# Second feed-forward matrix by seven block products per block of four, with operands summed beside the first matrix

## The chip, the core and the metric

The kernel runs on one core of a Trainium2 chip. The metric is the device time of one execution in microseconds (us). Three runs of the kernel before gave 3480.54, 3479.45 and 3491.56 us, median 3480.54 us. The engines are called as in the profile: PE is TensorE (matrix products), PEld its weight load, DVE VectorE, ACT ScalarE, POOL GpSimd, and SP the engine that here only issues DMA transfers.

## What is computed

One inference step of an encoder of two layers over 1056 tokens (1024 frames of a new stream and 32 of a running one). A layer mixes three kinds of attention, attends to a memory, and ends in a squared-ReLU feed forward between two norms:

```python
D_MODEL = 1024
DEPTH = 2
D_FF = 4 * D_MODEL
...
    x = layer_norm(ALPHA * x + memory_attention(x, mem_k, mem_v, w_xq, w_xo), ln_g[1], ln_b[1])
    ffn = jnp.square(jax.nn.relu(x @ w_ff1)) @ w_ff2
    x = layer_norm(ALPHA * x + ffn, ln_g[2], ln_b[2])
```

So the first matrix is 1024 by 4096, the second 4096 by 1024, both in each layer, in 32-bit floats.

## The kernel before

Activations lie transposed: features on the 128 partitions, tokens along the row, T = 1056. Every 32-bit product is three matmuls on rounded parts (`mm3`, L98 to L102): an operand x is split (`split`, L94 to L96) into hi, a rounded copy made by ACT (L95), and lo = x − hi, made by DVE (L96); the product is hi·hi + hi·lo + lo·hi. A raw weight chunk of 128x512 (256 KB) comes by a DMA on SP into a tile tagged "ws" (two buffers), and ACT and DVE split it into tiles "wu" (ring "w" of eight).

**First matrix** (`ffn_up`, L1419 to L1472). The 1024 inputs and the tokens are halved, which makes four blocks of the operand; the 4096 outputs go in 16 steps j of 256. In each j the eight block products are had from seven (the Strassen-Winograd scheme): `first_blocks` and `mix_blocks` (L1371 ff.) form the seven operands X once per layer, `mix_weights` (L1400 to L1417) sums the weights of every j: S1 and S2 on DVE (L1413, L1414), S3 and S4 on POOL (L1416, L1417), and splits all seven. A product is 24 matmuls of 128x264 (two halves of 264 tokens, four row blocks, three matmuls each). Results are combined on DVE (L1438, L1454), then made relu and squared on ACT (L1441, L1442), and stored to a DRAM buffer `hid` by DMAs on POOL's queue (L1444). A raw tile of mixed weights ("u" ring of large tiles, shared with Y) is loaded at L1404 and L1405.

**Second matrix** (`ffn_down`, L1474 to L1501). The 4096 rows go in eight groups: a group loads four hid rows from DRAM (SP), splits them, and multiplies with the weights of all eight output blocks in three chunks of 352 tokens (L100 to L102, `add_proj`, which adds into Y on DVE, L1212 and L1214). The last group goes chunk by chunk, with the second norm of the layer behind each chunk.

**Order.** A tile framework gives each engine its list by its own planner: instructions of one engine run in that order, and wait for semaphores of the others. SP alone keeps the order of the program. Tiles come from small pools of buffers, so a load also waits until its buffer's last reader is through.

## Time and profile before

| | us |
|---|---|
| runs | 3480.54, 3479.45, 3491.56 |
| profiled execution | 3483.91 |
| its span in the trace | 3482.1 |
| PE busy | 3318.6 (95%) |
| DVE busy | 2055.3 (59%) |
| ACT busy | 1524.9 (44%) |
| POOL busy | 464.6 (13%) |
| mean granted TensorE clock | 0.977 of full |

The page and the trace describe the one profiled execution. Busy is time in which an engine worked; register, branch, semaphore and DMA-issuing instructions don't count. A stretch's PEclk is the share of the full TensorE clock that was granted: 1.00 is 2.4 GHz, 0.50 is 1.2 GHz. In layer 1 the feed forward starts near 1015 us and its second matrix near 1362 us; layer 2 repeats this some 1700 us later.

### The profile page before, as it was taken

What the parts mean: (1) busy time and instruction counts of PE and PEld (TensorE: products, weight loads), DVE (VectorE), ACT (ScalarE), POOL (GpSimd) and SP (SyncE); (2) the same over time, 40 slices, a digit from 0 to 9 for tenths busy, and PEclk for the clock granted to TensorE, in tenths of its full rate; (3) what the DMA queues carried; (4) which work ended last, traced back from release to release, by engine and by line L of the source; (5) the groups of instructions that cost most, each with busy time, mean ns of one, the idle gap of its engine ahead of it and who ended that gap; (6) DMA issues with size and microseconds to landing.
All of it is one profiled execution on the core that took longest, in us unless ns stands there. A gap on an engine that the chain in (4) does not pass through costs nothing.

```text
span 3482.1 us, 61117 instructions
## 1 busy us (share of the span) xinstructions
PE 3318.6 (95%) x23904; PEld 3084.8 (89%) x23904; DVE 2055.3 (59%) x4223; ACT 1524.9 (44%) x3312; POOL 464.6 (13%) x722
## 2 busy tenths in 40 slices
PE   8999999999979999999989999999999799999998
PEld 6988879689879999999989887786898799999997
DVE  5666742566587665444656677335666866654446
ACT  5555533554555544221254554335544545431113
POOL 0101023110013221000011111221000232200000
PEclk9999999999989999999999999999999899999999
DMA  4424236432313334322143332455422233352221
GB/s 161 135 54 119 70 129 207 126 118 92 133 54 123 112 108 168 105 99 93 45 133 95 88 98 68 139 175 136 145 95 91 95 107 110 106 190 87 80 99 57
DMA packets 196425, 386.83 MB, mean 111 GB/s; under 512 B 46240, under 2 KB 98120, under 8 KB 195880
## 3 DMA queue, kind: packets, MB, share of 16 engines
q1 hardware_dynamic: 119600, 248.66, 22.8%
q0 software_dynamic: 41056, 125.63, 10.3%
q10 hardware_dynamic: 35480, 8.64, 1.3%
q8 instruction: 189, 3.10, 0.4%
q14 instruction: 100, 0.82, 0.1%
HBM read 259.60 MB, written 123.23 MB: 110 GB/s over the span
## 4 chain that ended last, share of the span: by engine, by line
PE 76%; DVE 7%; DMA 6%; issue 6%; ACT 3%; POOL 1%; SPq 0%; ACTq 0%; another core or an unknown queue 0%; DVEq 0%; POOLq 0%
PE psw L100 16%; PE psw L101 16%; PE psw L102 16%; PE pso L792 2%; PE pss L785 2%; PE pso L100 2%; PE pso L102 2%; PE pso L101 2%; PE pss L101 2%; PE pss L102 2%; PE pso L161 2%; PE pss L100 2%; DMA Gb<-gd 1%; DVE X L96 1%; PE pst L100 1%
## 5 line engine op out<-in xcount | busy, mean ns | idle before, releaser
L100 PE MATMUL psw<-X,wu 128*128 128x352 f32 (+1 forms) x2496 | 806.0, 323 | 33.2 <-ACT X L95 24.2
L101 PE MATMUL psw<-X,wu 128*128 128x352 f32 (+1 forms) x2496 | 798.2, 320 | 8.2 <-DVE X L96 8.0
L102 PE MATMUL psw<-X,wu 128*128 128x352 f32 (+1 forms) x2496 | 799.1, 320 | 4.4 <-DVE wu L96 4.1
L100 PEld LDWEIGHTS psw<-X,wu 128*128 128x128 f32 x2496 | 477.5, 191 | 44.0 <-ACT X L95 25.2
L100 PE MATMUL psw<-hid,wu 128*128 128x352 f32 x1536 | 500.2, 326 | 7.3 <-ACT wu L95 5.3
L101 PE MATMUL psw<-hid,wu 128*128 128x352 f32 x1536 | 498.7, 325 | 0.0
L102 PE MATMUL psw<-hid,wu 128*128 128x352 f32 x1536 | 497.7, 324 | 0.0
L101 PEld LDWEIGHTS psw<-X,wu 128*128 128x128 f32 x2496 | 476.5, 191 | 14.7 <-DVE X L96 9.5
L102 PEld LDWEIGHTS psw<-X,wu 128*128 128x128 f32 x2496 | 477.2, 191 | 7.7 <-DVE wu L96 5.4
L95 ACT CAST wu<-ws 128x512 fp32r<-128x512 f32 x304 | 182.3, 619 | 525.5 <-PE psw L101 379.7
L1214 DVE TENSOR_TENSOR Y<-psw,Y 128x352 f32<-128x352 f32 x336 | 175.3, 523 | 294.0 <-PE psw L102 290.9
L100 PEld LDWEIGHTS psw<-hid,wu 128*128 128x128 f32 x1536 | 289.8, 189 | 8.9 <-ACT wu L95 5.7
L101 PEld LDWEIGHTS psw<-hid,wu 128*128 128x128 f32 x1536 | 290.6, 189 | 0.5
L102 PEld LDWEIGHTS psw<-hid,wu 128*128 128x128 f32 x1536 | 289.8, 189 | 0.7
L96 DVE TENSOR_TENSOR wu<-ws,wu 128x512 fp32r<-128x512 f32 x304 | 204.6, 688 | 119.2 <-ACT wu L95 95.2
L96 DVE TENSOR_TENSOR wu<-wraw,wu 128x512 fp32r<-128x512 f32 x224 | 195.5, 878 | 77.1 <-ACT wu L95 77.0
L95 ACT CAST wu<-wraw 128x512 fp32r<-128x512 f32 x224 | 136.1, 617 | 158.2 <-PE pst L102 38.7
L180 ACT ACTIVATE lnq<-Y 128x352 f32<-128x352 f32 x168 | 76.9, 492 | 176.2 <-DVE Y L177 156.4
L1441 ACT ACTIVATE ff<-ff 128x528 f32<-128x528 f32 (+1 forms) x160 | 88.3, 554 | 122.2 <-DVE ff L1454 88.9
L1444 POOL DMA_DIRECT2D hid<-ff x160 | 87.1, 544 | 403.3 <-ACT ff L1442 270.2
L100 PE MATMUL pss<-X,wu 128*128 128x264 f32 x448 | 128.5, 288 | 3.1 <-ACT X L95 3.1
L101 PE MATMUL pss<-X,wu 128*128 128x264 f32 x448 | 128.6, 287 | 1.7 <-DVE X L96 1.7
(540 smaller groups left out, 6909.6 us busy)
## 6 DMA issues: line engine op xcount, KB each, us to landing
hid<-hid SPq DMA_DIRECT2D x64, 528.0 KB
wraw<-in_w_ff_dram SPq DMA_DIRECT2D x64, 512.0 KB
ws<-in_w_ff_dram SPq DMA_DIRECT2D x128, 256.0 KB
ws<-in_w_in_dram SPq DMA_DIRECT2D x100, 256.0 KB
hid<-ff POOLq DMA_DIRECT2D x96, 264.0 KB, 3.8
xd<-Y POOLq DMA_DIRECT2D x24, 704.0 KB, 3.9
Y<-xd SPq DMA_DIRECT2D x24, 704.0 KB
foxd<-fb POOLq DMA_DIRECT2D x24, 352.0 KB, 3.6
```

Source lines behind the costliest of these rows:

```text
L95: self.nc.scalar.copy(hi, src)
L96: (eng or self.nc.vector).tensor_sub(lo, src, hi.bitcast(F32))
L100: mm(ps, lhs[0], rhs[0], start=first, stop=False)
L101: mm(ps, lhs[0], rhs[1], start=False, stop=False)
L102: return mm(ps, lhs[1], rhs[0], start=False, stop=last)
L161: total = lambda ps, x, k=0, n=1: nc.tensor.matmul(ps[:, :CW], self.o1024, x, start=k == 0, stop=k == n - 1)
L180: nc.scalar.activation(q, y(k), AF.Square)
L785: nc.tensor.transpose(pt[:, c:c + 128], Ps[h][:, 128 * k:128 * k + 128], self.ident)
L792: nc.tensor.matmul(po[64 * h:64 * h + 64, 0:128], V[k][:, 64 * h:64 * h + 64], PT[:, k - k0, h], start=k == 0, stop=k == kts - 1)
L1214: nc.vector.tensor_add(y, ps, y)
L1441: nc.scalar.activation(x, x, AF.Relu)
L1444: nc.gpsimd.dma_start(self.hid[2 * j + i, :, n * HT + c * QT:n * HT + c * QT + m], x.rearrange("p c n -> p (c n)"))
```

## The change

The second matrix is done by seven block products too. Of the 16 pairs of its row blocks (outputs j of the first matrix), 14 (`FAST`) go this way; the last four hid rows are multiplied as before. In `ffn_down`, each of seven operands of 14 blocks of 528 tokens meets the four column blocks m: 14 · 3 · 2 = 84 matmuls of 128x264 for each, and the result is added into one to four blocks of Y (`to`).

- The operands are sums of results of the first matrix. They are formed in `ffn_up` by DVE right after the results, stored to a DRAM buffer `tp` (seven operands) by DMAs on ACT's queue and SP's, and read back by `down_operand`. `hid` shrinks to four rows and is stored through ACT's queue.
- The weight sums for the second matrix are made on POOL by `down_sums`: for each j from 2 on and each m a 256 KB load into a "ws" buffer, four sums of 128x128, and a 256 KB store into a buffer `sp`; 56 of them per layer. They are issued after the last operand sum of the first matrix (`issue_after`).
- S3 and S4 of the first matrix's weights move from POOL to DVE. The raw weights are loaded one j ahead.
- Products 0 and 1 of j = 0 to 3 (`EARLY`) are done ahead, in `ffn_first`, from unmixed operands; their results go to DRAM through POOL's queue and come back on SP's, and `ffn_up` has five products in those j. The order of products is now 0, 1, 2, 3, 6, 4, 5.
- Y is loaded back inside `ffn_down` in eight pieces; Xn is allocated at the first norm.

Over both layers 4032 matmuls of 128x352 go and 4704 of 128x264 come.

```diff
+FAST = 14
+EARLY = 4
...
-        sub(B21, B21, B22, self.nc.gpsimd)
+        for h in halves:
+            self.after = self.nc.gpsimd.tensor_sub(B21[:, h], B21[:, h], B22[:, h]).ins
...
+    def mix_weights(self, raw, first=False):
+        nc = self.nc
...
+        W = [None, None] if first else [split(A11), split(A12)]
         nc.vector.tensor_add(S1, A21, A22)
         nc.vector.tensor_sub(S2, S1, A11)
         W += [split(S2), split(S1)]
-        nc.gpsimd.tensor_sub(S3, A11, A21)
-        nc.gpsimd.tensor_sub(S4, A12, S2)
+        nc.vector.tensor_sub(S3, A11, A21)
+        nc.vector.tensor_sub(S4, A12, S2)
...
+    def ffn_first(self, l, X):
+        nc = self.nc
+        self.hid = self.dram("hid", [32 - 2 * FAST, 128, T])
+        self.tp = self.dram("tp", [7, FAST, 128, HT])
+        self.sp = self.dram("sp", [4, 4, 128, FAST, 128])
+        self.p1d = self.dram("p1d", [EARLY, 128, 2, QT])
+        for j in range(EARLY):
+            W = self.k3(self.unit(self.I["w_ff1"][l, 2 * j]), 8)
+            ps = self.block_product(lambda k: [a[:, k] for a in W], X[0])
+            p1 = self.tl("q", [128, 2, QT], name="ff")
+            for c in range(2):
+                nc.scalar.copy(p1[:, c], ps[c])
+            nc.gpsimd.dma_start(self.p1d[j], p1)
+            ps = self.block_product(lambda k: [a[:, 4 + k] for a in W], X[1])
+            c11 = self.tl("q", [128, 2, QT], name="ff")
+            for c in range(2):
+                nc.vector.tensor_add(c11[:, c], ps[c], p1[:, c])
+            self.squared(c11)
+            nc.gpsimd.dma_start(self.tp[0, j], c11.rearrange("p c n -> p (c n)"))
...
+    def down_sums(self, l, j):
+        eng = self.nc.gpsimd
+        last = None
+        def store():
+            if last:
+                eng.dma_start(self.sp[:, last[0], :, j].rearrange("s p n -> p s n"), last[1])
+        for m in range(4):
+            raw = self.tl("ws", [128, 4, 128], name="wb")
+            c0 = 512 * (m % 2) + 256 * (j % 2)
+            src = self.I["w_ff2"][l, j // 2, :, :, c0:c0 + 256].rearrange("(a u) p c -> u p a c", a=2)[m // 2]
+            eng.dma_start(raw.rearrange("p (a k) n -> p a (k n)", a=2), src)
+            store()
+            A11, A12, A21, A22 = (raw[:, i] for i in range(4))
+            eng.tensor_add(A22, A21, A22)
+            eng.tensor_sub(A21, A11, A21)
+            eng.tensor_sub(A11, A22, A11)
+            eng.tensor_sub(A12, A12, A11)
+            last = m, raw
+        store()
...
+                W = self.mix_weights(raw, j < EARLY)
+            if j < 15:
+                raw = self.raw_weights(I["w_ff1"][l, 2 * j + 2:2 * j + 4])
...
+                if j >= FAST:
+                    nc.scalar.dma_start(self.hid[2 * (j - FAST) + at[0], :, HT * at[1] + t0:HT * at[1] + t0 + n], flat(x))
+                elif i is not None:
+                    nc.scalar.dma_start(self.tp[i, j, :, t0:t0 + n], flat(x))
...
+            if j < EARLY:
+                nc.sync.dma_start(u, self.p1d[j])
+                for c in range(2):
+                    nc.sync.dma_start(flat(c11[c]), self.tp[0, j, :, c * QT:(c + 1) * QT])
+            else:
+                product(0)
+                for c in range(2):
+                    nc.scalar.copy(u[:, c], ps[c])
+                product(1)
+                for c in range(2):
+                    nc.vector.tensor_add(c11[c][:, 0], ps[c], u[:, c])
+                for c in range(2):
+                    square(c11[c], 0, (0, 0), c)
+            fast = j < FAST
+            product(2)
...
+            if fast:
+                for c in range(2):
+                    nc.vector.tensor_sub(c12[:, c], c12[:, c], c11[c][:, 0])
+                nc.sync.dma_start(self.tp[3, j], flat(c12))
+            product(4)
+            plus(c22, c22)
+            plus(u, u)
+            square(c22, 6, (1, 1))
+            if fast:
+                nc.vector.tensor_sub(c22, c22, c12)
+                nc.sync.dma_start(self.tp[2, j], flat(c22))
+                for c in range(2):
+                    nc.vector.tensor_sub(c11[c][:, 0], c22[:, c], c11[c][:, 0])
+                    nc.sync.dma_start(self.tp[4, j, :, c * QT:(c + 1) * QT], flat(c11[c]))
+            product(5)
+            plus(u, u)
+            square(u, 1, (1, 0))
+            if fast:
+                nc.vector.tensor_sub(u, u, c22)
+                nc.sync.dma_start(self.tp[5, j], flat(u))
+            if j >= 16 - FAST:
+                with self.tc.issue_after(self.after):
+                    self.down_sums(l, j - 16 + FAST)
...
+        def take(tile, n):
+            j = len(X)
+            lo, hi = tile
+            (self.nc.gpsimd if i else self.nc.sync).dma_start(lo.bitcast(F32), self.tp[i, j:j + n].rearrange("j p n -> p j n"))
+            for a in range(0, n, 2):
+                b = min(a + 2, n)
+                self.split(hi[:, a:b], lo[:, a:b], lo[:, a:b].bitcast(F32))
+            X.extend((hi[:, a], lo[:, a]) for a in range(n))
...
+                raw = self.tl("ws", [128, 4, 128], name="ws")[:, :b - a]
+                if i in (0, 1, 5):
+                    for k in range(a, b, 2):
+                        src = self.I["w_ff2"][l, (j0 + k) // 2, m // 2 + (i == 5) * 2]
+                        src = src.rearrange("p (m k e n) -> p m k e n", m=2, k=2, e=2)[:, m % 2, :, int(i > 0)]
+                        nc.sync.dma_start(raw[:, k - a:k - a + 2], src)
+                else:
+                    nc.sync.dma_start(raw, self.sp[{2: 0, 6: 1, 4: 2, 3: 3}[i], m, :, j0 + a:j0 + b])
+                self.split(hi[:, a:b], lo[:, a:b], raw)
...
+        to = [((0, 0), (0, 1), (1, 0), (1, 1)), ((0, 0),), ((0, 1), (1, 0), (1, 1)), ((0, 1), (1, 1)), ((1, 0), (1, 1)),
+              ((1, 0),), ((0, 1),)]
+        X = self.down_operand(0)
+        Y = None
+        for i in range(7):
+            for m in range(4):
+                W = self.down_weights(l, i, m)
+                if Y is None:
+                    Y = [self.tl("u", [128, 4, ROW], name="Y") for _ in range(2)]
+                    for k in range(4):
+                        for a in range(2):
+                            nc.sync.dma_start(Y[a][:, k, :T], xd[:, 4 * a + k])
+                if m == 0:
+                    Xn = self.down_operand(i + 1) if i < 6 else self.last_hid()
+                ps = {}
                 for c in range(2):
                     ps[c] = self.ps("wsowsowt"[self.nps % 8])[:, :QT]
                     self.nps += 1
...
+                    for k in range(FAST):
+                        self.mm3(ps[c], W[k], [x[:, c * QT:(c + 1) * QT] for x in X[k]], k == 0, k == FAST - 1)
+                for a, b in to[i]:
+                    for c in range(2):
+                        y = Y[a][:, m, HT * b + QT * c:HT * b + QT * (c + 1)]
+                        if i == 0:
+                            nc.vector.scalar_tensor_tensor(y, y, ALPHA, ps[c], ALU.mult, ALU.add)
+                        else:
+                            nc.vector.tensor_add(y, ps[c], y)
+            X = Xn
...
+        self.ffn_first(l, X)
+        W = self.mix_weights(self.raw_weights(I["w_ff1"][l, 0:2]), True)
```

Three places of the engines' lists follow; the changed kernel's line numbers are its own: L99 and L100 there are the two halves of `split`, L1505 is `plus`, L1421 to L1425 are S1 to S4.

POOL in layer 1 at the last operand sum before the first matrix (Y_9305 is half of the block sums, hid, tp and sp are DRAM buffers). Before:

```order
L1444 DMA hid_10405<-ff_10461 128x264
L1444 DMA hid_10405<-ff_10462 128x264
L1385 TENSOR_TENSOR Y_9305<-Y_9305 128x2x528 x2
L1444 DMA hid_10405<-ff_10525 128x528
L1416 TENSOR_TENSOR wraw_10624<-wraw_10624 128x512
L1444 DMA hid_10405<-ff_10526 128x528
L1444 DMA hid_10405<-ff_10432 128x528
L1417 TENSOR_TENSOR wraw_10624<-wraw_10624 128x512
L1416 TENSOR_TENSOR wraw_10870<-wraw_10870 128x512
```

After the change (L1397 is the operand sum, wb a "ws" tile):

```order
L1397 TENSOR_TENSOR Y_9305<-Y_9305 128x2x528
L1477 DMA wb_11245<-in_w_ff_dram 128x2x256
L1477 DMA wb_11251<-in_w_ff_dram 128x2x256
L1480 TENSOR_TENSOR wb_11245<-wb_11245 128x128
L1481 TENSOR_TENSOR wb_11245<-wb_11245 128x128
L1482 TENSOR_TENSOR wb_11245<-wb_11245 128x128
L1483 TENSOR_TENSOR wb_11245<-wb_11245 128x128
L1480 TENSOR_TENSOR wb_11251<-wb_11251 128x128
L1472 DMA sp_10340<-wb_11245 128x4x128
L1481 TENSOR_TENSOR wb_11251<-wb_11251 128x128
L1482 TENSOR_TENSOR wb_11251<-wb_11251 128x128
```

POOL's list was stores of results with a weight sum between them; it is now, from there on, pairs of load, load, eight sums, two stores.

DVE in layer 1 about the first steps j of the first matrix (ff are results, wraw raw weights and their sums, ps.. PSUM). Before, the combining of j = 0 and then the weights of j = 1:

```order
L1438 TENSOR_TENSOR ff_10526<-pso_10562,ff_10526 128x264
L1438 TENSOR_TENSOR ff_10526<-psw_10575,ff_10526 128x264
L1438 TENSOR_TENSOR ff_10432<-pss_10593,ff_10432 128x264
L96 TENSOR_TENSOR wu_10627<-wraw_10624,wu_10627 128x512
L1438 TENSOR_TENSOR ff_10432<-pso_10606,ff_10432 128x264
L96 TENSOR_TENSOR wu_10630<-wraw_10624,wu_10630 128x512
L1413 TENSOR_TENSOR wraw_10624<-wraw_10624 128x512
L1414 TENSOR_TENSOR wraw_10624<-wraw_10624 128x512
L1413 TENSOR_TENSOR wraw_10870<-wraw_10870 128x512
L96 TENSOR_TENSOR wu_10635<-wraw_10624,wu_10635 128x512
```

After the change (wraw_10691 holds the weights of j = 1; L1544 is a parked sum):

```order
L1421 TENSOR_TENSOR wraw_10691<-wraw_10691 128x512
L1424 TENSOR_TENSOR wraw_10691<-wraw_10691 128x512
L1505 TENSOR_TENSOR ff_10694<-psw_10700,ff_10694 128x264
L1505 TENSOR_TENSOR ff_10694<-pss_10713,ff_10694 128x264
L1505 TENSOR_TENSOR ff_10754<-pso_10728,ff_10694 128x264
L1505 TENSOR_TENSOR ff_10754<-psw_10741,ff_10694 128x264
...
L1544 TENSOR_TENSOR ff_10783<-ff_10783,ff_10696 128x264
L1505 TENSOR_TENSOR ff_10694<-psw_10830,ff_10694 128x264
L1422 TENSOR_TENSOR wraw_10691<-wraw_10691 128x512
L1505 TENSOR_TENSOR ff_10694<-pss_10843,ff_10694 128x264
L1425 TENSOR_TENSOR wraw_10691<-wraw_10691 128x512
L100 TENSOR_TENSOR wu_10865<-wraw_10691,wu_10865 128x512
```

S1 and S3 of j = 1 now stand ahead of the first results of j = 0, and S2, S4 and the splits of j = 1 between and behind its last results.

ACT in layer 1 at the end of the first matrix (wu<-ws are casts of the second matrix's weights). Before:

```order
L1441 ACTIVATE ff_14216<-ff_14216 128x528
L95 CAST hid_14334<-hid_14334 128x1056
L1442 ACTIVATE ff_14216<-ff_14216 128x528
L95 CAST hid_14334<-hid_14334 128x1056
L95 CAST wu_14342<-ws_14343 128x512
L1441 ACTIVATE ff_14122<-ff_14122 128x528
L95 CAST wu_14342<-ws_14347 128x512
L1442 ACTIVATE ff_14122<-ff_14122 128x528
```

After the change (X_14941 and X_14945 are row blocks of operand 1 of the second matrix, ff_14632 and ff_14631 among the first and the last results of j = 15):

```order
L1439 ACTIVATE ff_14632<-ff_14632 128x264
L99 CAST X_14941<-X_14941 128x528
L1440 ACTIVATE ff_14632<-ff_14632 128x264
L99 CAST X_14945<-X_14945 128x528
L1511 DMA hid_10338<-ff_14632 128x264
...
L1439 ACTIVATE ff_14631<-ff_14631 128x528
L1511 DMA hid_10338<-ff_14750 128x528
L1440 ACTIVATE ff_14631<-ff_14631 128x528
L99 CAST wu_14905<-ws_14906 128x512
L1511 DMA hid_10338<-ff_14631 128x528
L99 CAST wu_14905<-ws_14911 128x512
```

Casts of operand 1 now stand among the squares of j = 15, and the first weights of the second matrix behind the last square.

## Rows read from the trace of the kernel before

**Rows 1.** The page's head and its busy times by engine (share of the span, instructions).

```profile
span 3482.1 us, 61117 instructions
...
PE 3318.6 (95%) x23904; PEld 3084.8 (89%) x23904; DVE 2055.3 (59%) x4223; ACT 1524.9 (44%) x3312; POOL 464.6 (13%) x722
```

**Rows 2.** Windows, steady stretches: window, length, busy (count) of PE, PEld, DVE, ACT, POOL; clock, DMA, GB/s.

```profile
1150.00:1200.00 50.00, 50.00 (x412) 50.00 (x411) 29.32 (x54) 26.02 (x49) 12.76 (x17) 1.00 0.36 122
...
1100.00:1300.00 200.00, 200.00 (x1642) 200.00 (x1641) 125.57 (x229) 98.65 (x187) 54.62 (x68) 1.00 0.30 103
...
1420.00:1700.00 280.00, 280.00 (x1736) 279.92 (x1736) 130.03 (x217) 48.75 (x68) 0.00 (x0) 1.00 0.25 85
```

**Rows 3.** Windows, the start of the feed forward of layer 1.

```profile
1004.00:1015.00 11.00, 9.68 (x53) 7.56 (x52) 7.43 (x7) 6.17 (x11) 0.00 (x0) 1.00 0.14 52
1015.00:1027.00 12.00, 1.95 (x14) 1.60 (x12) 9.42 (x12) 7.58 (x15) 2.60 (x4) 0.77 0.36 127
1027.00:1042.00 15.00, 9.20 (x37) 8.28 (x38) 15.00 (x12) 5.48 (x7) 6.79 (x2) 0.50 0.04 14
1042.00:1048.00 6.00, 6.00 (x51) 6.00 (x51) 5.03 (x6) 2.54 (x3) 0.00 (x0) 1.00 0.25 76
```

**Rows 4.** Timeline of SP: the raw weights of the next step j.

```profile
1045.55 0.33 SPq L1404 DMA_DIRECT2D wraw<-in_w_ff_dram  x1
```

**Rows 5.** Windows, from the first matrix to the second in layer 1.

```profile
1362.00:1364.00 2.00, 1.64 (x7) 1.61 (x8) 2.00 (x3) 1.90 (x4) 0.00 (x0) 0.69 0.17 61
1364.00:1366.00 2.00, 2.00 (x8) 2.00 (x8) 0.28 (x1) 0.00 (x0) 0.54 (x1) 0.50 0.47 163
```

**Rows 6.** Timeline of PE there: start, duration, instruction, idle before and its releaser.

```profile
1362.36 0.43 PE L100 MATMUL psw<-hid,wu 128*128 128x352 f32 x1 [2.62 <-ACT wu L95]
```

**Rows 7.** Timeline of DVE and POOL in one step j of the first matrix.

```profile
1150.14 0.68 DVE L96 TENSOR_TENSOR wu<-wraw,wu 128x512 fp32r<-128x512 f32 x1
...
1158.62 1.76 POOL L1416 TENSOR_TENSOR wraw<-wraw 128x512 f32<-128x512 f32 x1 [1.10 <-DMA wraw<-in_w_ff_dram]
...
1159.16 1.77 DVE L96 TENSOR_TENSOR wu<-wraw,wu 128x512 fp32r<-128x512 f32 x1
1160.86 0.42 DVE L1454 TENSOR_TENSOR ff<-psw,ff 128x264 f32<-128x264 f32 x1
```

**Rows 8.** Groups of DVE, 1100 to 1300 us: the split of weights (busy, mean ns).

```profile
L96 DVE TENSOR_TENSOR wu<-wraw,wu 128x512 fp32r<-128x512 f32 x70 | 62.8, 897 | 25.9 <-ACT wu L95 25.9
```

**Rows 9.** DMA issues: KB each, median us from issue to landing.

```profile
hid<-ff POOLq DMA_DIRECT2D x96, 264.0 KB, 3.8
...
kvd<-mkv POOLq DMA_DIRECT2D x8, 256.0 KB, 3.7
```

**Rows 10.** Groups of POOL, whole span.

```profile
L1417 POOL TENSOR_TENSOR wraw<-wraw 128x512 f32<-128x512 f32 x32 | 42.2, 1318 | 46.1 <-DVE wraw L1414 46.1
...
L765 POOL COPY ri<-sm 128x128 f32<-128x128 f32 x64 | 19.9, 313 | 61.4 <-DVE sm L764 27.1 <-ACT sPT L839 8.3 <-DVE sm L748 8.1
```

**Rows 11.** Timeline of ACT where weights come through the two "ws" buffers alone.

```profile
765.73 0.62 ACT L95 CAST wu<-ws 128x512 fp32r<-128x512 f32 x1 [2.69 <-DMA ws<-in_w_out_dram]
...
770.01 0.62 ACT L95 CAST wu<-ws 128x512 fp32r<-128x512 f32 x1 [2.73 <-DMA ws<-in_w_out_dram]
...
774.15 0.62 ACT L95 CAST wu<-ws 128x512 fp32r<-128x512 f32 x1 [2.50 <-DMA ws<-in_w_out_dram]
```

**Rows 12.** Windows, the stretch with the most transfers that was looked at.

```profile
1340.00:1350.00 10.00, 10.00 (x84) 10.00 (x84) 1.73 (x4) 3.39 (x8) 1.62 (x3) 1.00 1.04 371
```

164 lines of the change are left out of this document (87 added, 77 removed).

## The prediction

> **What bounds the kernel now.** I read the page first. PE is busy 3318.6 of 3482.1 us, DVE 2055.3, POOL 464.6 [rows 1]: TensorE is the bound of the whole, so fewer matmuls shorten the time only where PE still gets its operands. The windows give the pace at full clock [rows 2]. In the first matrix 412 matmuls of 264 columns are recorded in 50.0 us, 121.4 ns each; in the second 1736 of 352 columns in 280 us, 161.3 ns each. I take 121.2 and 160.8, since a few records can be missing. In both stretches PE is busy all the time; nothing else shows up there. DVE works 125.6 of 200 us in the first, 130.0 of 280 in the second.
>
> PE stands idle at two places per layer. At the start of the feed forward [rows 3] it is busy 1.95 of 12 us, then 9.20 of 15 us at a granted clock of 0.50 while DVE is busy without a gap (15.00 of 15). At the change of matrix [rows 5, 6] it waits 2.62 us for an ACT cast of weights and then runs two windows at 0.69 and 0.50.
>
> **PE's saving.** 4032 matmuls of 352 columns go: 4032 × 160.8 ns = 648.3 us. 4704 of 264 columns come: 4704 × 121.2 ns = 570.1 us. Difference 78.2 us, 39.1 per layer, all of it in the second matrix, where PE is the path. The rest of the sum is what that is reduced by.
>
> **Start of the feed forward.** Early products (4 j × 2 products × 24 = 192 matmuls, 23.3 us of PE) go into a stretch where some 21.5 us per layer are lost: from 1004 to 1048 us 155 matmuls are recorded, 16 of them the norm's, where full pace would give many more [rows 3]. Some 144 of them fit, 17.5 us. Against it: DVE is full there, and the early products bring eight evictions and their splits, about 4 us longer; then the order puts S1 and S3 of j = 1 ahead of every result of j = 0. Their raw weights could be loaded only once a Y slot is free, which before was at 1045.55 us [rows 4]; with 3 to 4 us of transfer and two DVE sums PE runs dry for an estimated 9 us, plus 2 us at half clock. S2, S4 and the first splits of j = 2 and j = 3 stand behind the results of the product before the last, 2.8 + 1.8 us each time. 17.5 − 4 − 11 − 2 × 4.6 = about −7; with part of those waits lying beside the j = 0 to 3 loads, I take −1 us per layer, range −8 to +13. So the early work buys nothing.
>
> **Steps j from 4 on.** PE needs 7 × 24 × 121.2 ns = 20.4 us for one. DVE spends 125.57/200 × 20.4 = 12.8 us on it now [rows 2]. About 1.45 us of that is waiting that shows as length: the weight split takes 897 ns on average [rows 8] where an undisturbed one takes 0.68, and the one beside a POOL sum 1.77 [rows 7]. Added: S3 and S4, 2 × 0.68 = 1.36; parked sums, four of 264 columns at 0.42 [rows 7] and two of 528 at about 0.7, 3.0 us. So 12.8 − 1.45 + 1.36 + 3.0 = 15.7 us. POOL now sums without a break: in 20.4 us two pairs, 16 sums. If each holds up DVE by 0.45 us that is 7.2, in all 22.9 > 20.4; but POOL waits for transfers most of the time, so I take 2 to 4 and 17.5 to 19.7 us. PE stays the bound, at a margin of 0.7 to 2.9 us.
>
> Queues: four stores per j move from POOL to ACT, which is busy 98.65 of 200 us [rows 2]; at 0.33 us an issue [rows 4] that is 1.3 us per j, beside PE. SP gets five stores per j, each waiting for a DVE sum, with the raw weights of a later j queued behind the last; these are needed only a whole j (20.4 us) on, so I cost both at nothing. Without that cover (a slot freed late) one landing of 3.8 us per j would show.
>
> By the Trainium skill, "SBUF — State Buffer", section "Who interferes with whom", a VectorE instruction with two SBUF inputs contends with a GpSimd instruction that reads SBUF, and the second blocks fully until the first is through. The 1.77 us beside 0.68 in this trace agrees. By that rule alone every meeting of two such sums costs the whole of one, which is the time of rival B.
>
> **POOL's sums.** A pair is load, load, eight sums, two stores, and the next loads wait for those stores (two "ws" buffers). Period: one load to landing, five sums (four and the first of the other tile), one store to landing. A 256 KB transfer issued from POOL lands after 3.7 to 3.8 us [rows 9]. A 128x128 sum isn't in these rows: from below a 128x128 copy, 0.31 us, from above a 128x512 sum, 1.32 [rows 10]; I take 0.5, nearer the one of equal size, with a second operand. 3.8 + 2.5 + 3.8 = 10.1 us (bounds 9.2 and 14.2). 28 pairs of a layer: 284 us, from about 1043 (the second block sum is through at the end of the third window [rows 3]) to 1327. They must be done by about 1346: behind them on POOL's queue stand the loads of operand 1, whose casts ACT has among the squares of j = 15, and "ws" is also what the second matrix's first weights need. So 19 us are to spare; they are late above 10.8 us a pair.
>
> By the Trainium skill, "DMA: Bandwidth & Descriptors", section "Anatomy of one DMA", a transfer of this kind costs about 2.0 us and its bytes over 436e3 per us: 2.6 us for 262,144 bytes. With 2.6 a pair would take 7.7 us and the sums end by about 1259, with more to spare and the total unchanged. The trace differs (3.7 us [rows 9]) and decides.
>
> **Change of matrix.** Now the first weights of the second matrix are cast behind the last square of j = 15, where one cast was ahead of it; the first step needs four chunks, of which two come only when "ws" is free again. Now 2.62 us idle and 1.8 at half clock are lost [rows 5, 6], 4.4 us. After the change I estimate 3.1 idle for the longer tail, 1.4 for the second pair of chunks and 1.8 + 1.4 at half clock, about 3.3 us more per layer. Y, loaded in eight pieces, waits beside it.
>
> **Second matrix.** A step m is 84 × 121.2 ns = 10.2 us and needs four weight chunks through two "ws" buffers. Where weights come this way alone two chunks take 770.01 − 765.73 = 4.3 us and 4.1 after it [rows 11], so 8.4 us for four: it fits, with 1.8 us to spare, and SP must also bring operands of 14 blocks (3.8 MB each, one per four steps m). I allow 4 us of stalls per layer (0 to 8), the waits behind operands loaded on POOL's queue among them. Traffic in the first matrix rises from 103 GB/s [rows 2] to an estimated 245: per j 1.0 MB of raw weights, 2.1 MB in and out of POOL's sums and 1.9 MB of parked operands in 20.4 us; under the 371 GB/s once moved with PE at full pace [rows 12]. Additions into Y on DVE: 112 per layer at 0.42 us [rows 7], 47 us in some 285 of PE, no bound.
>
> **The sum.** Per layer +39.1 − 1 (start) − 0.3 (reloads of parked results) − 3.3 − 4 − 1 (order of products, queues) = 29.5; both layers 59 us. 3483.9 − 59 = 3425 for a profiled execution, which was 3.4 above the median: **3422 us** (−1.7%).
>
> **Rivals.**
>
> *A. The early products pay.* If the raw weights land before PE runs dry, the start gives +13 per layer and the second matrix loses 2 instead of 8: 2 × (13 + 37) = 100 us, 3382. For it: PE's 10 idle us [rows 3] are there for the taking. Against it: the order of DVE shown. 0.15.
>
> *B. DVE bound in the first matrix.* If POOL's sums hold up DVE at each turn, a step takes 22.9 us: 2.5 × 12 × 2 = 60 us go back and the time is 3482, no change. For it: 1.77 us [rows 7]. Against it: POOL waits for DMA in three quarters of a pair. 0.10.
>
> *C. POOL's sums come late, and it is slower.* From 10.8 us a pair on, the second matrix waits for them; the gain of 29.5 is eaten at 1346 + 29.5 = 1375.5, which is (1375.5 − 1043)/28 = 11.9 us a pair. At 12.5 us (sums of 0.7, and 4.5 us per transfer, as the queues fill at 245 GB/s) the end is 1393, 47 us late per layer: 3422 + 94 = 3516. For it: mean length of a sum unknown, the lock that lengthens POOL's as well (1.76 us [rows 7]), more traffic. Against it: 19 us to spare, few other transfers beside POOL's own. 0.13.
>
> **Chances and range.** Forecast 0.62, A 0.15, B 0.10, C 0.13. What a measurement can tell from no change is about 0.5%, 17 us: 3463 to 3498. Faster by more: forecast and A, 0.77, with the part of B that ends a little better, 0.78; within: the rest of B, 0.09; slower: C, 0.13. The forecast's own range by the bounds of its terms is 3392 to 3452 (start −8 to +13, stalls 0 to 8, change of matrix 0 to 7). A reaches to 3380, B to 3490; about 2 in 10 lie outside, C above all. Range 3380 to 3490.
>
> **What would show it.** In the changed profile: PE busy lower by about 78 us; steps j of 20.4 us with PE full from j = 4 on, DVE at 17 to 20 of them (B: PE idle for DVE casts there); POOL's last "sp" store about 285 us after the first load of "wb", before the last squares of the first matrix (C: PE waits behind the load of operand 1 or of sums, and the second matrix starts late); a gap of some 9 us before the second step j (A: none); 84 matmuls per 10.2 us in the second matrix without idle PE. The forecast is wrong if POOL's pairs take over 10.8 us, or if the weights of a step m take longer than 10.2.

## The result and the profile after

The changed kernel takes 3587.41 us in the median (3583.03 to 3599.97), the one before 3486.05 us over the runs of that comparison: a ratio of 1.0293, 95% interval 1.0266 to 1.0321. It is slower by 2.9%, some 101 us. The forecast was 3422 us, range 3380 to 3490; the time lies outside. The direction is that of rival C, by more than its price.

The page of the changed kernel, head and busy times (before: [rows 1]):

```profile
span 3581.1 us, 64268 instructions
...
PE 3291.8 (92%) x24576; PEld 3039.3 (85%) x24576; DVE 2166.2 (60%) x4535; ACT 1615.8 (45%) x3488; POOL 788.2 (22%) x1290
```

PE works 27 us less and the span is 99 us longer: it waits more. (78 us less had been forecast; part of the matmuls ran at a lower granted clock, 0.67 to 0.91 in most of the windows below.) Windows of the changed kernel in layer 1, in the first matrix and at the change of matrix (columns as in rows 2):

```profile
1100.00:1120.00 20.00, 15.53 (x110) 15.24 (x111) 12.67 (x25) 5.99 (x11) 12.15 (x19) 0.89 0.73 242
...
1140.00:1160.00 20.00, 20.00 (x167) 20.00 (x166) 14.52 (x31) 9.77 (x19) 11.49 (x18) 1.00 0.70 227
...
1240.00:1260.00 20.00, 16.75 (x124) 16.36 (x123) 11.05 (x23) 6.50 (x13) 10.75 (x17) 0.91 0.61 196
...
1380.00:1400.00 20.00, 10.44 (x86) 10.22 (x84) 2.83 (x7) 3.23 (x6) 9.97 (x19) 0.89 0.82 287
1400.00:1420.00 20.00, 7.13 (x36) 6.90 (x36) 14.06 (x25) 14.75 (x25) 6.88 (x12) 0.67 0.76 255
1420.00:1440.00 20.00, 13.23 (x84) 12.71 (x84) 12.43 (x21) 6.23 (x10) 0.00 (x0) 0.76 0.76 277
1440.00:1460.00 20.00, 16.98 (x125) 16.95 (x126) 7.54 (x16) 4.33 (x8) 0.00 (x0) 0.83 0.35 99
```

At full pace such a window holds 165 to 167 matmuls of 264 columns. The first matrix loses matmuls in most of its windows (from 1140 to 1200 us it keeps its pace), at the change of matrix the three windows from 1380 us hold 206 where 498 would fit, and the second matrix begins some 60 us later than before (1422.8 against 1362.4 us, [rows 6]). What ends last there is told by the chain of waits of the changed kernel (start, duration, what):

```profile
1384.29 6.76 DMA sp<-wb
...
1392.24 5.49 DMA wb<-in_w_ff_dram
...
1400.14 2.97 DMA sp<-wb
...
1403.72 7.84 DMA ws<-in_w_ff_dram
```

It is GpSimd's weight sums, load after store after load, until 1403 us, and then the second matrix's first weights. From 1039.0 to 1400.1 us GpSimd makes 28 pairs, **12.9 us a pair**, where I had 10.1. One half of a pair, GpSimd's timeline of the changed kernel:

```profile
1091.04 0.71 POOL L1477 DMA_DIRECT2D wb<-in_w_ff_dram  x1
1096.42 0.72 POOL L1477 DMA_DIRECT2D wb<-in_w_ff_dram  x1 [4.67 <-DMA sp<-wb]
1097.36 0.46 POOL L1480 TENSOR_TENSOR wb<-wb 128x128 f32<-128x128 f32 x1 [0.22 <-DMA wb<-in_w_ff_dram]
...
1099.74 0.78 POOL L1472 DMA_DIRECT2D sp<-wb  x1 [0.30 <-POOL wb L1483]
```

GpSimd's groups from 1039 to 1401 us (busy, mean ns, idle time before them) give the whole ledger of the 28 pairs:

```profile
L1472 POOL DMA_DIRECT2D sp<-wb x56 | 43.4, 775 | 18.0 <-POOL wb L1483 15.7 <-issue 2.3
L1477 POOL DMA_DIRECT2D wb<-in_w_ff_dram x56 | 40.2, 718 | 69.2 <-DMA sp<-wb 64.6 <-issue 4.6
L1482 POOL TENSOR_TENSOR wb<-wb 128x128 f32<-128x128 f32 x56 | 36.3, 649 | 4.4
L1481 POOL TENSOR_TENSOR wb<-wb 128x128 f32<-128x128 f32 x56 | 34.6, 618 | 4.3
L1483 POOL TENSOR_TENSOR wb<-wb 128x128 f32<-128x128 f32 x56 | 33.7, 601 | 4.4
L1480 POOL TENSOR_TENSOR wb<-wb 128x128 f32<-128x128 f32 x56 | 30.3, 542 | 43.1 <-DMA wb<-in_w_ff_dram 42.5
```

A pair holds 3.0 us of issues (two loads, two stores), 4.8 us of sums (eight, 0.60 us each on average; one alone is 0.46), 3.8 us of waiting for transfers and 1.3 us of small gaps. My sum followed one tile through a load, five sums of 0.5 us and a store. But GpSimd does the sums and the issues of both tiles one after the other. A landing is counted from the start of its issue (3.8 us for a load, 3.3 for a store in the median), so the issue of that transfer is inside it; what I left out is three of the eight sums and the issues for the other tile. The page before has such issues (the hid stores, 0.54 us each); I counted them as a queue's, not as GpSimd's time.

Behind the sums stand the loads of operand 1, as the order showed; ACT meets their casts amid the squares of j = 15:

```profile
1384.15 0.38 ACT L1525 COPY ff<-psw 128x264 f32<-128x264 f32 x1
1405.25 0.63 ACT L99 CAST X<-X 128x528 fp32r<-128x528 f32 x1 [20.72 <-DMA X<-tp]
```

### The profile page after: what moved, and what is told of

It is laid out like the page before. It is cut to its first block, busy times and chain, and to the rows that moved or that the text cites. A ratio compares the mean times of both kernels' runs of the same rounds, so it can differ in the third digit from the quotient of the medians.

```text
span 3581.1 us, 64268 instructions
## 1 busy us (share of the span) xinstructions
PE 3291.8 (92%) x24576; PEld 3039.3 (85%) x24576; DVE 2166.2 (60%) x4535; ACT 1615.8 (45%) x3488; POOL 788.2 (22%) x1290
## 4 chain that ended last, share of the span: by engine, by line
PE 45%; DMA 23%; issue 9%; POOL 9%; DVE 8%; ACT 4%; SPq 1%; ACTq 0%; POOLq 0%; DVEq 0%
PE psw L104 9%; PE psw L105 9%; PE psw L106 8%; DMA wb<-in_w_ff_dram 7%; DMA sp<-wb 4%; DMA ws<-sp 4%; DMA ws<-in_w_ff_dram 3%; PE pso L796 2%; POOL wb L1482 2%; PE pss L789 2%; DVE wu L100 2%; POOL wb L1481 2%; DVE X L100 2%; POOL wb L1483 2%; PE pso L165 2%
## 5 line engine op out<-in xcount | busy, mean ns | idle before, releaser
L104 PE MATMUL psw<-X,wu 128*128 128x352 f32 (+1 forms) x3084 | 982.6, 319 | 71.5 <-ACT wu L99 31.6
L105 PE MATMUL psw<-X,wu 128*128 128x352 f32 (+1 forms) x3084 | 971.2, 315 | 13.6 <-DVE X L100 13.6
L106 PE MATMUL psw<-X,wu 128*128 128x352 f32 (+1 forms) x3084 | 971.9, 315 | 8.3 <-DVE wu L100 8.0
L104 PEld LDWEIGHTS psw<-X,wu 128*128 128x128 f32 x3084 | 594.2, 193 | 87.4 <-ACT wu L99 36.5
L105 PEld LDWEIGHTS psw<-X,wu 128*128 128x128 f32 x3084 | 593.7, 193 | 21.5 <-DVE X L100 15.4
L106 PEld LDWEIGHTS psw<-X,wu 128*128 128x128 f32 x3084 | 593.8, 193 | 13.2 <-DVE wu L100 11.0
L100 DVE TENSOR_TENSOR wu<-ws,wu 128x512 fp32r<-128x512 f32 (+1 forms) x432 | 276.8, 654 | 371.1 <-ACT wu L99 344.0
L99 ACT CAST wu<-ws 128x512 fp32r<-128x512 f32 (+1 forms) x432 | 251.1, 592 | 544.0 <-DMA ws<-in_w_ff_dram 205.0
L104 PE MATMUL pso<-X,wu 128*128 128x264 f32 x840 | 247.3, 295 | 64.0 <-DVE ff L1528 36.5
L106 PE MATMUL pso<-X,wu 128*128 128x264 f32 x840 | 246.7, 294 | 19.1 <-DVE wu L100 19.1
L104 PE MATMUL pss<-X,wu 128*128 128x264 f32 x840 | 243.8, 291 | 14.0 <-DVE ff L1505 7.5
L105 PE MATMUL pso<-X,wu 128*128 128x264 f32 x840 | 244.2, 291 | 2.0 <-DVE X L100 2.0
L106 PE MATMUL pss<-X,wu 128*128 128x264 f32 x840 | 241.2, 287 | 0.3 <-DVE wu L100 0.3
L105 PE MATMUL pss<-X,wu 128*128 128x264 f32 x840 | 241.4, 287 | 0.0
L104 PEld LDWEIGHTS pso<-X,wu 128*128 128x128 f32 x840 | 163.8, 195 | 69.4 <-DVE ff L1528 37.7
L100 DVE TENSOR_TENSOR wu<-wraw,wu 128x512 fp32r<-128x512 f32 x208 | 153.3, 756 | 85.3 <-ACT wu L99 85.1
L99 ACT CAST wu<-wraw 128x512 fp32r<-128x512 f32 x208 | 118.6, 615 | 147.2 <-DVE wraw L1422 66.0
L106 PEld LDWEIGHTS pso<-X,wu 128*128 128x128 f32 x840 | 163.9, 195 | 22.8 <-DVE wu L100 22.6
L104 PEld LDWEIGHTS pss<-X,wu 128*128 128x128 f32 x840 | 161.0, 192 | 17.9 <-ACT wu L99 7.8
L105 PEld LDWEIGHTS pso<-X,wu 128*128 128x128 f32 x840 | 164.1, 195 | 2.2 <-DVE X L100 2.2
L106 PEld LDWEIGHTS pss<-X,wu 128*128 128x128 f32 x840 | 160.8, 191 | 0.5 <-DVE wu L100 0.5
```

The source lines that it names most:

```text
L99: self.nc.scalar.copy(hi, src)
L100: (eng or self.nc.vector).tensor_sub(lo, src, hi.bitcast(F32))
L104: mm(ps, lhs[0], rhs[0], start=first, stop=False)
L105: mm(ps, lhs[0], rhs[1], start=False, stop=False)
L106: return mm(ps, lhs[1], rhs[0], start=False, stop=last)
```

## The experiments

Times are medians, ratios are to the kernel before in the same comparison with their 95% interval. Kernels are compared with 3587 (the change) or with 3471 (the change without sums). The kernel before took 3479 to 3486 us in these comparisons, so where two medians are subtracted the difference of the ratios stands beside it.

### 1. Without the sums

```diff
-            if j >= 16 - FAST:
-                with self.tc.issue_after(self.after):
-                    self.down_sums(l, j - 16 + FAST)
```

> The changed kernel without GpSimd's weight sums (no load, sum or store of them); the second matrix reads raw weights of the same size instead, so the products of four of its seven operands use unsummed weights. Theory 1 (GpSimd's sums, 12.9 us a pair, end some 60 us after PE could have gone on): the last result of the first matrix moves from 1420 to about 1360 us in layer 1, and the time falls from 3587 by 110 to 150 us, to 3440 to 3475. Rival 2 (the first matrix itself is slow: the start, parked sums and their stores, DVE): it stays above 3530. Rival 3 (the second matrix is held up by its weights through two buffers): the second matrix still takes over 375 us from its first matmul to the end of its norm, where 355 were forecast.

Measured: 3470.8 us (0.9951, 0.9928 to 0.9975). The sums cost 117 us (119 by the ratios), within what theory 1 gave. Rival 3 holds beside it, by this measure: from its first matmul to the last store of its norm the second matrix takes 394 us (1363.5 to 1757.8), nearly the 403 of the kernel before. Windows of this kernel:

```profile
1160.00:1180.00 20.00, 20.00 (x166) 20.00 (x165) 14.18 (x31) 8.83 (x18) 0.00 (x0) 1.00 0.39 140
...
1340.00:1360.00 20.00, 13.24 (x109) 13.02 (x108) 13.49 (x23) 12.77 (x20) 2.93 (x5) 0.95 1.02 371
1360.00:1380.00 20.00, 12.80 (x84) 12.28 (x84) 12.21 (x21) 6.93 (x11) 0.00 (x0) 0.76 0.81 290
```

From 1100 to 1340 us PE runs at full pace, though the parked sums and their stores are all there: beside them alone VectorE has time enough (14.5 of 20 us busy). But 3471 is far above 3422, so more of the forecast is wrong than the sums; experiments 3 and 4 take that apart.

### 2. Loads and stores without the sums between

```diff
-            eng.tensor_add(A22, A21, A22)
...
-            eng.tensor_sub(A12, A12, A11)
```

> The changed kernel with the loads and stores of GpSimd's weight sums, but without the sums between them (unsummed weights are stored). Of the 12.9 us of a pair eight sums are 4 to 5 us. Theory 1, if the sums themselves set the pace: a pair takes 8 to 9 us, the chain ends by about 1300 us in layer 1, and the time is within 15 us of the kernel without loads and stores too. If the transfers and their issue set it: a pair stays above 11 us and the time above 3540. If VectorE being locked out by the sums is what costs: PE's idle time in the first matrix goes, whatever the pair takes.

Measured: 3526.6 us (1.0126, 1.0089 to 1.0162), about halfway: 56 us above the kernel without transfers, 61 below the change. A pair takes 8.8 us, as theory 1 had it, but the time misses its 15 us. So loads, stores and their issue make 8.8 of the 12.9 us (I had 7.6 for them), and the sums between add 4.1 (I had 2.5). GpSimd's last store is issued at 1285.5 us, in good time, and still PE loses in the first matrix while the transfers run:

```profile
1220.00:1240.00 20.00, 17.12 (x124) 16.48 (x124) 11.01 (x23) 7.28 (x15) 6.49 (x9) 0.91 0.77 237
...
1300.00:1320.00 20.00, 20.00 (x167) 20.00 (x166) 13.51 (x29) 9.87 (x19) 0.00 (x0) 1.00 0.42 149
```

From 1100 to 1280 us PE is 197 matmuls short of full pace here, 149 in the changed kernel. So lateness is not the whole of it, and VectorE being locked out by sums isn't what holds PE up there: no sum runs.

### 3. Without the products ahead

```diff
-EARLY = 4
+EARLY = 0
...
```

With the sums:

> The changed kernel with no products ahead: all seven products in every step j. Theory 1 (GpSimd's chain, which starts at the same operand sum, ends the first matrix whatever PE does): within 15 us of the changed kernel, 3570 to 3605. Rival (the early products pay for themselves): 25 to 45 us slower, 3612 to 3632. My forecast's own step (they buy nothing): no change.

Without them:

> The kernel without GpSimd's sums (products of four operands use unsummed weights), and without products ahead. My forecast's step (the early products gain 17 us and lose as much at the first three steps j): within 10 us of 3471. Rival A (they pay 13 us a layer or more): 3495 or more. Rival (they cost more than they bring, as the 27 us of the kernel with sums hint): below 3455.

Measured: 3557.9 (1.0222, 1.0175 to 1.0269) and 3444.1 us (0.9887, 0.9852 to 0.9922). The products ahead don't buy nothing, they cost 29 and 27 us (25 and 22 by the ratios). With the sums that was outside every expectation, and it is at the edge of what the comparison tells; without them it is clear. Without the sums PE runs 271 matmuls in the 40 us from 1060 on with the products ahead, 331 when nothing was done ahead (windows of the two kernels); the gaps at steps 1 to 3 are larger than I had them.

```profile
1060.00:1080.00 20.00, 16.89 (x123) 16.27 (x122) 13.37 (x29) 6.23 (x11) 0.00 (x0) 0.91 0.49 178
1080.00:1100.00 20.00, 18.17 (x148) 17.77 (x146) 12.56 (x27) 6.36 (x11) 0.00 (x0) 1.00 0.55 185
```

```profile
1060.00:1100.00 40.00, 40.00 (x331) 40.00 (x330) 30.25 (x64) 19.66 (x39) 0.00 (x0) 1.00 0.41 144
```

### 4. The second matrix

Y in four parts:

```diff
-                    for k in range(4):
-                        for a in range(2):
-                            nc.sync.dma_start(Y[a][:, k, :T], xd[:, 4 * a + k])
+                if i == 0:
+                    for a in range(2):
+                        nc.sync.dma_start(Y[a][:, m, :T], xd[:, 4 * a + m])
```

> The kernel without GpSimd's sums (products of four operands use unsummed weights), and Y is read back in four parts, two pieces of 528 KB with each of the first four steps m, where all eight pieces stood together ahead of the weights of the second step. If those pieces, 4.2 MB in front of the next weights, make PE's wait of 10.2 us in the second step (1370 to 1381 us) and the half clock behind it: that wait falls to 0 to 4 us and the time by 14 to 28 us, from 3471 to 3443 to 3457. Rival (the weights through two buffers are late by themselves): the wait stays over 7 us and the time within 8 us.

Five buffers for raw weights ("q" holds results in the first matrix):

```diff
-                raw = self.tl("ws", [128, 4, 128], name="ws")[:, :b - a]
+                raw = self.tl(("ws", "ws", "q", "q", "q")[self.nraw % 5], [128, 4, 128], name="ws")[:, :b - a]
+                self.nraw += 1
```

> The kernel without GpSimd's sums (products of four operands use unsummed weights), and the second matrix takes its raw weights through five buffers (the two of before and three that hold results in the first matrix) in place of two. If two buffers hold up the second matrix (12.4 us of PE's waits from 1410 to 1700 us, 155 matmuls fewer than at full pace, 18.8 us): these waits fall under 4 us per layer and the time by 20 to 38 us, from 3471 to 3433 to 3451. Rival (the transfers themselves are slow, because operands of 3.8 MB pass at the same time): less than 10 us.

Measured: 3458.6 us (0.9931, 0.9902 to 0.996), 12 less than 3471 (7 by the ratios; the intervals overlap, so it can't be told from no change), and 3426.5 us (0.9834, 0.9803 to 0.9866), 44 less (41). PE's waits for the weights without sums (1340 to 1410 us), then with Y in parts (1320 to 1400, and one line of 1400 to 1700):

```profile
PE psw L104 <- ACT wu L99: 10.2, 1, 10.2
PE pso L104 <- ACT wu L99: 6.0, 1, 6.0
```

```profile
PE psw L104 <- ACT wu L99: 10.5, 1, 10.5
```

```profile
PE psw L104 <- ACT wu L99: 6.9, 2, 5.1
```

The expectation had put the long wait at the second step. By PE's timeline it stands before the first matmul of the second matrix (1363.5 us); the second step's wait is the one of 6.0 us (1382.5). That one is gone with Y in parts, but waits of 1.8 and 5.1 us stand at later steps. The long one ends with the cast of the first weights on ACT. That cast stands behind the last squares and behind the casts of operands 0 and 1, the first of these below waiting until its operand's load landed (without sums; not tested by a run of its own):

```profile
1352.02 4.62 ACT L99 CAST X<-X 128x1056 fp32r<-128x1056 f32 x6 [3.52 <-DMA X<-tp]
...
1362.82 0.60 ACT L99 CAST wu<-ws 128x512 fp32r<-128x512 f32 x1
```

Five buffers bring more than expected. With them the second matrix has no wait but one of 1.9 us from 1400 to 1700 us:

```profile
1420.00:1460.00 40.00, 40.00 (x331) 40.00 (x330) 20.69 (x36) 15.81 (x28) 6.08 (x11) 1.00 0.54 181
1460.00:1500.00 40.00, 40.00 (x331) 40.00 (x330) 23.73 (x47) 13.25 (x22) 3.33 (x5) 1.00 0.55 188
```

### 5. Sums made ahead

28 of 56 in the attention loops (`next(sums)` after each block), then 24 of 56 in the memory attention:

> The changed kernel with half of GpSimd's weight sums (28 of 56 per layer) made ahead, one after each block of the attention loops, the other half after the last operand sum as before. Theory 1: the second half ends near 1230 us, well before the second matrix, and the time is within 30 us of the kernel without sums: 3440 to 3500. Rival 2: above 3530. Rival (the sums disturb attention as much as the first matrix): attention grows by over 30 us per layer and nothing is gained.

> The changed kernel with 24 of the 56 weight sums of a layer made ahead on GpSimd in the memory attention, one after each of its steps, where GpSimd has next to nothing else; the other 32 as before. Theory 1: they end near 1250 us and come in time, 16 pairs of 12.9 us from 1040 on; the memory attention grows by under 10 us a layer; the time falls from 3587 by 80 to 115 us to 3470 to 3510. Rival (the sums cost what they cost, wherever they stand, by transfers and by holding up VectorE): over 3550, as in the run with half of them in the attention loops (3658).

Measured: 3658.4 (1.0496, 1.0455 to 1.0537) and 3618.4 us (1.0381, 1.0349 to 1.0414): both slower than the change, and both with a wait of their own. PE's and ACT's waits, the first line of the kernel with sums in attention (500 to 1000 us), the others of that with sums in the memory attention (760 to 1060):

```profile
PE pso L801 <- POOL ri L771: 32.0, 6, 10.0
```

```profile
PE psw L106 <- ACT mP L1282: 43.8, 3, 41.9
...
ACT wu L101 <- DMA ws<-in_w_xo_dram: 48.8, 6, 41.9
```

In attention GpSimd has copies that PE waits for, and they stand behind a load that waits for a buffer. In the memory attention the output weights come through the two buffers that the sums occupy. In the second kernel the 16 pairs were over near 1300 us (1250 expected), and from 1320 us on the first matrix ran at full pace; so theory 1 holds there, but the price was moved.

### 6. Repairs with the sums left in

`e9_sp_rows` stores a sum tile in one piece; `e10_three` has no products ahead, Y in parts and other weight buffers; `e11_all` has these, and raw operands first:

```diff
-        for i in range(7):
+        todo = (0, 1, 5, 2, 6, 4, 3)
+        for at, i in enumerate(todo):
...
-            (self.nc.gpsimd if i else self.nc.sync).dma_start(lo.bitcast(F32), self.tp[i, j:j + n].rearrange("j p n -> p j n"))
+            (self.nc.gpsimd if at > 1 else self.nc.sync).dma_start(lo.bitcast(F32), self.tp[i, j:j + n].rearrange("j p n -> p j n"))
```

> The changed kernel with another layout of the DRAM buffer of the weight sums: each sum tile is stored in one piece of 2 KB per partition (before four of 512 B), and read back in pieces of 512 B. If the small pieces of the stores, on engines that are 65 to 75% busy there, are what lengthens a pair and PE's waits in the first matrix: a pair falls from 12.9 to 11 to 12 us and the time from 3587 by 20 to 50 us. Rival (latency of one transfer after another and the issue on GpSimd's queue, whatever the pieces): a pair above 12.4 us and the time within 15 us.

> The changed kernel with the three repairs that helped without the sums: no products ahead, Y read back in four parts, weights of the second matrix through three other buffers at first and five later. The sums stay as they are. If the terms add up: 3587 - 27 - 12 - 44 = 3504, range 3490 to 3530. Rival (the sums' chain hides them, since it ends the first matrix anyway): above 3540.

> The same three repairs, the sums stored in one piece, and the operands of the second matrix in the order 0, 1, 5, 2, 6, 4, 3, so that the three that take raw weights come first and the sums are needed some 120 us later; operand 1 comes on SP's queue, not behind the sums on GpSimd's. If lateness of the chain is most of what the sums cost: 3430 to 3475, faster than the kernel before. Rival (what they cost is PE's waits all along the first matrix, by transfers and VectorE): 3480 to 3520.

Measured: 3574.8 (1.0264, 1.0239 to 1.0289), 3508.9 (1.0071, 1.0044 to 1.0098) and 3499.1 us (1.0051, 1.0036 to 1.0067). In one piece a store takes 0.575 us to issue and a pair 12.4 us (12.8 in `e11_all`); the 13 us gained can't be told from no change, since the intervals overlap. The three repairs bring 79 us with the sums in (77 by the ratios), where they had brought 27 + 12 + 44 = 83 without (70 by the ratios): they add up as far as the comparisons tell. Making the sums' lateness harmless brings 10 more at most (the intervals overlap), and the time stays 76 us above what follows in 7. With all of it the second matrix runs at full pace from 1440 us on, but the first loses 45 us per layer between 1100 and 1400 (373 matmuls short of 166 per 20 us, at 121 ns).

### 7. What loses those 45 us

`e12_no_park` leaves out the parked sums on VectorE and their stores; `e13_defer` makes 20 of 56 weight sums in the second matrix:

> The kernel with all repairs (3499 us), without the parked sums of results on VectorE and their stores to DRAM; the four operands concerned read other parked results instead. GpSimd's sums stay. In the kernel with all repairs PE loses some 45 us per layer from 1100 to 1400 us, its waits end with VectorE instructions that wait for a parked store to free one of three result buffers. If that is the cause: the loss falls under 15 us per layer, the first matrix takes 20.4 us a step, and the time falls by 50 to 90 us, to 3410 to 3450. Rival (GpSimd's sums hold up VectorE's splits themselves, or the raw weights land late): the loss stays above 30 us a layer, the time above 3470.

> The kernel with all repairs, and 20 of the 56 sums of a layer made in the second matrix, while its first three operands, which take raw weights, are multiplied. If PE's loss in the first matrix goes with the sums that run beside it: 5/14 of 45 us per layer come back, 25 to 35 us in all, and the time is 3465 to 3475, some 0.3% faster than the kernel before. Rival (the loss is moved into the second matrix, or the sums come late there): 3490 or more.

Measured: 3423.1 us (0.9829, 0.9806 to 0.9852) and 3503.9 (1.0056, 1.0033 to 1.0079), no gain over 3499. The first is clear: without parked sums PE runs at full pace beside GpSimd's sums.

```profile
1140.00:1180.00 40.00, 40.00 (x331) 40.00 (x330) 24.85 (x50) 20.11 (x38) 26.52 (x46) 1.00 0.55 190
1180.00:1220.00 40.00, 40.00 (x331) 40.00 (x330) 24.45 (x50) 20.12 (x38) 24.26 (x43) 1.00 0.55 187
```

GpSimd is busy for 24 to 26 of 40 us there, and VectorE's work fits. In the first matrix parked stores without weight sums cost PE nothing (1), and weight sums without parked stores nothing either; together they do. The run takes out the sums, the stores and their traffic at once (203 GB/s from 1100 to 1340 us in `e11_all`, 176 here), so it doesn't say which of them. VectorE's waits of `e11_all` (1060 to 1340 us) point to one way (in total, times, longest):

```profile
DVE ff L1559 <- DMA tp<-ff: 25.2, 9, 4.0
DVE ff L1550 <- DMA tp<-ff: 14.8, 11, 3.0
DVE ff L1527 <- DMA tp<-ff: 10.0, 8, 3.2
```

A parked sum is made in place of a result whose store still runs, and a store of 264 KB on SP's queue lands after 3.7 us in the changed kernel, after 2.3 without the sums (medians of the whole run):

```profile
tp<-ff SPq DMA_DIRECT2D x84, 264.0 KB, 3.7
```

```profile
tp<-ff SPq DMA_DIRECT2D x84, 264.0 KB, 2.3
```

Two runs moved the in-place sums away from the stores on VectorE's list, three gave them places of their own in the raw weight tile (`spare`):

```diff
-                nc.vector.tensor_sub(c22, c22, c12)
-                nc.sync.dma_start(self.tp[2, j], flat(c22))
+                nc.vector.tensor_sub(spare[0], c22, c12)
+                nc.sync.dma_start(self.tp[2, j], flat(spare[0]))
...
```

> The kernel with all repairs (3499 us), and the parked sums c22 - c12 and c11 moved on VectorE's list from behind product 4 to behind product 5 of each step j. These sums are made in place and wait until the store of the value before them has been read out (VectorE waited for stores of parked results 50 us from 1060 to 1340 us in that kernel); what stands behind them on VectorE, PE's evictions, waits too. If that order is the mechanism: the loss of 45 us per layer in the first matrix falls by a third to two thirds, the time to 3440 to 3475. Rival (the stores hold buffers, wherever the sums stand): 3485 or more.

> As the run before, and the sum u - c22 moved behind the evictions of product 1 of the next step j as well, so that VectorE meets none of the stores while they run. If the order on VectorE is the mechanism: 5 to 30 us less than the run before, 3425 to 3460, a version faster than the kernel before. Rival (the buffer of u is now held for longer and the next step's results wait for it): slower than the run before.

> The kernel with all repairs (3499 us), and the parked sums are written into dead parts of the step's raw weight tile, not over the results they are made from; nothing is left out. Moving the sums on VectorE's list gave 0 and 11 us, and the waits only changed their place (to the two tiles of the first result and to the results' buffers): so it is the buffers that the stores hold. If so: PE's loss in the first matrix falls under 10 us per layer, as in the run without parked sums, and the time to 3420 to 3445, faster than the kernel before by 1 to 1.8%. Rival (the transfers as such, slow beside GpSimd's): above 3480.

> The changed kernel with that one thing alone: parked sums in dead parts of the raw weight tile. GpSimd's chain of sums still ends the first matrix there (near 1400 us in layer 1), so PE's shorter waits before it count for little: 3550 to 3585. Rival (the held buffers are most of the loss of the change): 3490 to 3520.

> The kernel with all repairs, and the parked sums in those parts of two fixed raw weight tiles that held S1 to S4, which the next loads don't overwrite; nothing is left out. In the run before with parked sums in the raw tile the waits for parked stores went from VectorE's list, but the raw weights then waited for these stores (45 us on SP's queue) and ACT for the raw weights (74.5 us). If held buffers, wherever they lie, are what costs: both waits go, PE's loss from 1060 to 1360 us falls under 10 us a layer and the time to 3420 to 3450, faster than the kernel before. Rival (transfers are slow beside GpSimd's, and something always waits for them): 3475 or more.

Measured: 3501.4 (1.004, 1.0019 to 1.006), 3488.3 (1.0014, 1.0 to 1.0027), 3494.5 (1.0042, 1.0026 to 1.0057), alone in the changed kernel 3568.0 (1.0235, 1.0206 to 1.0265), and 3509.3 us (1.0074, 1.0053 to 1.0095). All but the fourth missed what I hoped for, and the traces show another wait in the old one's place. From 1060 to 1340 us, where 2324 matmuls would fit, PE runs 1976 in `e11_all`, 2001 and 2049 with the sums moved, 2017 and 2022 with places of their own: each gives back a part at most. In `e15_later_park` VectorE waits 38.5 us for the stores of c11's two tiles. In `e18_spare_s` it waits for no parked store any more, but SP's queue has the raw weights behind the last parked store of the step, and ACT and VectorE have the splits at the start of the next. ACT's waits there (1060 to 1380 us), then one of them in the timelines of SP and ACT:

```profile
ACT wu L99 <- DMA wraw<-in_w_ff_dram: 53.7, 13, 5.1
```

```profile
1193.87 0.32 SPq L1562 DMA_DIRECT2D tp<-wraw  x1
1194.24 1.66 SPq L1407 DMA_DIRECT2D wraw<-in_w_ff_dram  x2
```

```profile
1200.88 0.62 ACT L99 CAST wu<-wraw 128x512 fp32r<-128x512 f32 x1 [4.45 <-DMA wraw<-in_w_ff_dram]
```

What a version would take that has neither wait was not tried. So it isn't shown that held buffers are the cause; the rival, transfers that land late beside GpSimd's whatever waits for them, is not excluded. No version that leaves nothing out is faster than the kernel before; `e15_later_park` is level with it.

## Why the prediction was wrong

**PE's saving: right.** 331 matmuls per 40 us in the repaired second matrix are 120.8 ns each, as counted. In the kernel without sums and with five buffers PE is busy for 3246.8 us, 72 less than before, where 78 were forecast.

**POOL's sums: the step that failed first.** "Period: one load to landing, five sums (four and the first of the other tile), one store to landing" gave 10.1 us; measured 12.9. The chain of one tile left out what GpSimd does for the other one meanwhile. By experiment 2 transfers and issues are 1.2 us above my figure and the sums 1.6. Nor does POOL wait for transfers "in three quarters of a pair": it is 3.8 of 12.9 us. The forecast's own bounds held the period (9.2 to 14.2), and its own condition (late above 10.8, no gain from 11.9 on) then gives rival C: 1043 + 28 × 12.9 = 1404, 58 us late per layer, 3422 + 116 = 3538. The place and the mechanism of C were right (the loads of operand 1, ACT's cast amid the squares of j = 15); its price lacked what the sums do before they are late. Of the 117 us that the sums cost, 61 went when the sums between were left out and the chain was through in time, and 56 only with its transfers (2).

**Steps j from 4 on: wrong in what bounds them.** VectorE's busy time was not the limit: per step of 168 matmuls it is 15.8 us from 1100 to 1340 us, where I had 17.5 to 19.7. So rival B's lock did not decide: without any sum on GpSimd PE lost as much (2), and with the sums but no parked stores nothing (7). By the Trainium skill, "SBUF — State Buffer", section "Who interferes with whom", a VectorE instruction with two SBUF inputs contends with a GpSimd one that reads SBUF. The first sums of the changed kernel, 1.36 us where one alone takes 0.46, agree with it.

**Queues: the second step that failed.** The stores on ACT's and SP's queues and the raw weights behind them were priced at nothing: "these are needed only a whole j (20.4 us) on, so I cost both at nothing". The lists of ACT and VectorE have the splits of those weights at the start of the next step, and the parked sums wait in place for their own stores. I had priced the loss of the cover ("one landing of 3.8 us per j would show"), and about that was lost: 45 us per layer in the repaired kernel, some 3 us a step. That it goes with the parked stores is shown (7); through which of the waits it is lost stays open, as does why the changed kernel keeps its pace from 1140 to 1200 us.

**Start: right in mechanism, wrong in size.** The gap at step 1 came where I had told it, 5.1 us and not 9 (without sums: PE waits for VectorE, whose sum waits 3.8 us for raw weights). I took −1 us per layer against nothing done ahead; measured −11 to −15. My terms gave "about −7", and the step from there to −1 had no row behind it.

**Change of matrix and second matrix: mis-sized.** For the change I had 4.5 us of idle time and 3.3 more per layer than before. Without sums PE waits 10.2 us for the first weights and 6.0 for the second step's (4). My sum had the weights alone; on ACT their cast stands behind those of operands 0 and 1. For the second matrix I had 4 us of stalls per layer; two buffers cost 20 to 22, since two chunks took about 5 us and not 4.2 with pieces of 128 KB and operands beside them.

**The sum of it.** 3587 − 117 (sums) − 83 (products ahead, Y, buffers) = 3387 (3393 by the ratios), below my 3422, if they add up as they did in 6; this sum was not run.

**The transfers' price.** By the Trainium skill, "DMA: Bandwidth & Descriptors", section "Anatomy of one DMA", a transfer issued from GpSimd costs about 2.0 us and its bytes over 436e3 per us, an estimate of 2.6 us for 256 KB. The medians here are 3.8 for the loads and 3.3 for the stores, so the trace differs, and the 3.7 to 3.8 us of the rows were nearer.

## What to carry to other kernels

When work is moved onto an idle engine, count all that the engine does for it, the issue of each transfer among it, and divide the time to the deadline by that: 28 pairs had 303 us and needed 361. A tile that is stored and then changed in place puts the store's landing on the engine's list, and what stands behind it there waits too (VectorE waited 50 us per layer so); so does a load behind a store on a queue in program order. Take such a change apart by leaving out one part at a time: parked stores and weight sums each left PE at full pace in the first matrix, and together they cost 76 us.

## What the runs showed of the hardware

The issue of a 256 KB store kept GpSimd for 0.775 us in four pieces per partition and for 0.575 us in one; a load of 256 KB for 0.72. GpSimd's 128x128 sum took 0.46 us alone, 0.60 on average and 1.36 where VectorE was busy. With GpSimd's transfers beside them (the DMA engines 65% busy from 1100 to 1340 us, 43% without) parked stores of 264 KB landed after 3.7 us where they took 2.3, and raw weights of 512 KB after 6.0 where they took 5.0.
